# From up to down projection: the last block's product and sums on VectorE, two weight tiles placed elsewhere, two weight sums a step later

## The chip, the cores and the metric

One core of a Trainium2 chip runs the whole kernel in one launch. The core has TensorE (matrix products, PE in the profile, with the weight loads of its array as PEld), VectorE (DVE), ScalarE (ACT), GpSimd (POOL) and SyncE (SP), which here only issues DMAs. The metric is the device time of one execution in microseconds; the figure for the kernel before is the median of three runs.

## The reference

One layer of a diffusion backbone: a modulated norm, an mLSTM group and a windowed attention group, an output projection, and a channel mixer. The change lies in the channel mixer, for 1024 tokens, model width 1024 and hidden width 2816:

```python
def conv_glu(h, w_up, conv_w, conv_b, w_down):
    a, val = jnp.split(h @ w_up, 2, axis=-1)
    a = jax.nn.gelu(dwconv(a, conv_w, conv_b))
    return (a * val) @ w_down
...
        x = x + g_f * conv_glu(modulate(rmsnorm(x, norm_ffn[l]), sh_f, sc_f),
                               w_up[l], ffn_conv_w[l], ffn_conv_b[l], w_down[l])
...
    return rmsnorm(x, final_norm)
```

## The kernel before

**Up projection.** The 22 blocks of 128 hidden columns run in the loop over `i` from line 1773 on. For each block TensorE makes the gate and value rows, VectorE adds the parts and applies the convolution's taps, ScalarE does the gelu, and the product gate times value is made in two halves of 512 tokens: `mul1` on VectorE (line 1724) and `mul2` on GpSimd (line 1727), both into the block's tile `tt`. A block is held back by one turn, so the product of block 20 is made while TensorE works on block 21. The last block, `i = NF - 1 = 21`, is finished behind the loop, at lines 1904 to 1928.

**What is stored.** The down projection is done by a Strassen-like scheme with seven products instead of eight, so it needs sums of quarters of the hidden activation. `combine` (line 1730) stores a block's halves to DRAM and, for the second block of each couple, makes three sums on GpSimd, stores each (s1, s2, s4), with the partner block's tile `p` as room. It stores with `put`, which issues a DMA on SP. The helpers `add` (line 1496) and `sub` (line 1210) give the sums their lines in the profile. The third sum writes `tt[:, h1]`, the half that the a11/a12 store reads.

**Down projection.** Seven products follow in the order m1, m6, m2, m7, m5, m4, m3. Each goes through 11 blocks of 128 rows of weights, taken in six pairs (the sixth has one block). One pair of one product is a *step*, numbered n = 0 to 41, six to a product: m1 is steps 0 to 5, m6 is 6 to 11. A step is 24 matmuls (12 for a sixth pair): for each block of the pair and each of four row groups, three matmuls (line 2032), because both operands are split into a high and a low half. The first matmul of the three takes high and high, the second the low half of the weights (`dl`), the third the low half of the left operand (`al`).

A step's operands are prepared ahead, in an order that is written out by hand for TensorE, VectorE, ScalarE, GpSimd and SP alike, each of which works through it in order. In step n:

- `load(n + 4)` issues the weight load and the loads of the left operand (tiles `ar`, three of them in rotation) on SP;
- `cut(n + 2)` splits: ScalarE casts to the high half (line 1372: `dh` for weights, `ah` for the left operand), VectorE subtracts it from the source (line 1373: `dl`, `al`). At step 0 nothing is cut: the operands of steps 0 to 2 are split before the loop, those of step 3 in step 1.

**Weight sums.** m6, m7 and m4 use sums and differences of weight quarters. The dictionary `sums` says at which step the sum of pair j is due: steps 2, 3, 4, 6, 7, 8 for pairs 0 to 5. Two steps before its key, the loads of `b22[j]` and of a row tile `br` are issued, 512 KB each (256 KB for the sixth pair); at the key, behind the cut, VectorE subtracts `br` from `b22[j]`; a step later, ahead of the cut, it adds `b22[j]` to `b11[j]`, which m6 takes from step 6 + j on.

**Memory.** Weight tiles `b11` of pairs 4 and 5 and all six `b22` lie in the pool `gt`. It begins where the up projection's split weights ended and covers the bytes of that stage's working tiles (`u2`, `u3`, `av`, `sn`, `tt`, `vt`, `s3`) and, further on, of the hidden input `hB`. A load into such bytes waits until their last reader is done. The order of allocation sets which tile lies where.

Of the kernel before, what the change touches and what calls it, by code (L numbers as in the profile page):

```python
# [13 lines left out]
ALU = mybir.AluOpType  # L14
# [18 lines left out]
NF = FF // P  # L33
# [45 lines left out]
def build(tc, I, out, dbg=None):  # L79
    nc = tc.nc  # L80
    dbg = dbg or {}
    V, S, G, T = nc.vector, nc.scalar, nc.gpsimd, nc.tensor
# [991 lines left out]
    class Wout:  # L1074
# [32 lines left out]
        def add(self, n):  # L1107
            ns = slice(512 * n, 512 * n + 512)
            V.tensor_tensor(out=self.xb[:, ns], in0=self.po[:], in1=self.xb[:, ns], op=ALU.add)
            if n == 1:  # L1110
                nc.sync.dma_start(x2_d[self.b][:], self.xb[:])
# [98 lines left out]
    sub = lambda e, o, x, y: e.tensor_tensor(out=o, in0=x, in1=y, op=ALU.subtract)  # L1210
# [62 lines left out]
    add = lambda e, o, x, y: e.tensor_tensor(out=o, in0=x, in1=y, op=ALU.add)  # L1273
# [15 lines left out]
    for t in range(n + 2):  # L1289
# [3 lines left out]
        if t in WOT:  # L1293
            k = 4 + WOT.index(t)
# [201 lines left out]
    add = lambda e, o, x, y: e.tensor_tensor(out=o, in0=x, in1=y, op=ALU.add)  # L1496
# [87 lines left out]
    f = ExitStack()  # L1584
# [84 lines left out]
    h1, h2_ = slice(0, 512), slice(512, 1024)  # L1669

    class Block:
# [52 lines left out]
            V.tensor_tensor(out=self.tt[:, h1], in0=self.a[:], in1=self.tt[:, h1], op=ALU.mult)  # L1724

        def mul2(self):
            G.tensor_tensor(out=self.tt[:, h2_], in0=self.vt[:], in1=self.tt[:, h2_], op=ALU.mult)  # L1727


        def combine(self):  # L1730
            tt, put = self.tt, lambda n, src: nc.sync.dma_start(act_d[n, self.m % KD][:], src)
            put(("a11", "a12")[self.m >= KD], tt[:, h1])
            if self.m < KD:
                s3 = fs.tile([P, 512], F32, name="s3", tag="s3", bufs=1)
                sub(G, s3[:], tt[:, h1], tt[:, h2_])
                put("s3", s3[:])
                return
            put("a22", tt[:, h2_])
            p = self.before.tt
            add(G, p[:, h2_], p[:, h2_], tt[:, h2_])  # L1740
            put("s1", p[:, h2_])
            sub(G, p[:, h1], p[:, h2_], p[:, h1])
            put("s2", p[:, h1])
            sub(G, tt[:, h1], tt[:, h1], p[:, h1])
            put("s4", tt[:, h1])

    def wblock(k, d, kt):
# [113 lines left out]
    NP = len(PAIRS)  # L1861
    pair = lambda pool, n, **kw: pool.tile([P, 2, 512], F32, name=n, **kw)
    b11 = [er] + [pair(gb, f"b11_{k}") for k in range(1, 4)]
# [69 lines left out]
    gt = g.enter_context(tc.tile_pool(name="gt", bufs=1, reuse_waits="tile"))  # L1933
# [1 line left out]
    bank = [pD.tile([P, 512], F32, name=f"pd{i}") for i in range(8)]  # L1935

    bank = [[bank[i] for i in sl] for sl in ((1, 2, 7, 3), (5, 6, 4, 0))]
    b11 += [pair(gt, f"b11_{k}") for k in range(4, NP)]
    b22 = [pair(gt, f"b22_{k}") for k in range(NP)]
    gfr = go.tile([P, D], F32, name="gfr")  # L1940
    fnr = go.tile([P, D], F32, name="fnr")
    us = [go.tile([P, 512], F32, name=f"us{i}") for i in range(4)]
# [90 lines left out]
                     skip_group_check=not fresh)  # L2033

    todo = []
    sums = {(2, 3, 4, 6, 7, 8)[j]: j for j in range(NP)}
    rows = {}
    for t, (p, ps, fresh) in enumerate(products):
        for j in range(NP):
# [12 lines left out]
            if n - 1 in sums:  # L2052
                k = sums[n - 1]
                m = len(PAIRS[k])
                add(V, b11[k][:, 0:m], b22[k][:, 0:m], b11[k][:, 0:m])
            if n + 2 in raws:
                q, k = steps[n + 2]
# [10 lines left out]
            if n in sums:  # L2068
                k = sums[n]
# [125 lines left out]
```

## Time and profile before

| what | value |
|---|---|
| median of three runs | 1264.26 us (1264.09 to 1265.34) |
| profiled execution, its own time | 1263.85 us |
| its span, first to last instruction | 1262.1 us |
| granted TensorE clock, mean | 0.999 |
| first matmul of the down projection starts at | 1043.68 us |
| last matmul of the down projection starts at | 1254.5 us |

The times in the profile count from the start of the span. A row of the instructions in order of time gives start, duration, engine, line, operation, output and inputs with their shapes, and in brackets how long the engine was idle before it and what ended that idle time. A row of the chain of work gives start, duration, engine or DMA and the tile. A row of the windows gives, for a stretch, its length, then the busy time of PE, PEld, DVE, ACT and POOL with the count of instructions, the granted clock, the share of DMA engines in use and GB/s. Matmuls are pipelined: their durations overlap, so a matmul's lateness is read from the distance of the starts.

### The profile page before, as it was taken

To read this page: it belongs to the slowest core of one execution; us is meant where nothing else is said; L and a number is where in the kernel's file an instruction comes from. 1 tells how busy PE (TensorE), PEld (TensorE's weight loads), DVE (VectorE), ACT (ScalarE), POOL (GpSimd) and SP (SyncE) were. 2 spreads that over 40 slices of the span, in tenths; PEclk is the share of its full clock that TensorE was granted. 3 is DMA by queue.
4 is the path that set the end of the run, shared out by engine and by line. 5 is a ranking of instruction groups with operands and counts; after the bars stand their busy time and mean duration, and the time that the engine had idled before them with its cause. 6 is when DMAs were issued, how large, how long until landed. Compare 5 with 4: busy or idle time off the path is not lost.

```text
span 1262.1 us, 19247 instructions
## 1 busy us (share of the span) xinstructions
PE 1233.2 (98%) x7044; PEld 1059.5 (84%) x7044; DVE 973.4 (77%) x1691; ACT 638.8 (51%) x1310; POOL 187.5 (15%) x162
## 2 busy tenths in 40 slices
PE   6999999999999999999999999999999999999997
PEld 4799999999898888888887888888888888788886
DVE  5863777777887888788987877777777777877887
ACT  6732556464865777776843333333333334434435
POOL 1200000000001444221002232133231232001000
PEclk9999999999999999999999999999999999999999
DMA  9541635352254333104314322223322237975563
GB/s 360 190 138 35 151 117 152 119 178 68 85 176 165 128 126 110 51 34 167 117 51 133 116 98 104 93 101 116 103 105 100 94 136 269 335 252 187 192 195 134
DMA packets 90560, 176.17 MB, mean 140 GB/s; under 512 B 12954, under 2 KB 29538, under 8 KB 90466
## 3 DMA queue, kind: packets, MB, share of 16 engines
q1 hardware_dynamic: 90178, 174.15, 41.1%
q8 instruction: 56, 0.92, 0.3%
q10 hardware_dynamic: 288, 0.79, 0.2%
q14 instruction: 38, 0.31, 0.1%
HBM read 136.58 MB, written 38.33 MB: 139 GB/s over the span
## 4 chain that ended last, share of the span: by engine, by line
PE 80%; DVE 7%; ACT 5%; DMA 5%; issue 2%; SPq 1%; POOL 1%; ACTq 0%; DVEq 0%; POOLq 0%
PE pd L2032 14%; PE pa L1492 8%; PE pc L1492 8%; PE pp L600 7%; PE pe L1492 4%; PE pd L1492 4%; PE pb L1492 4%; PE u L1194 3%; PE pv L305 2%; PE pv L307 2%; PE pv L306 2%; DMA wa<-in_w_ada_dram 2%; PE pt L1171 2%; PE po L305 2%; PE po L307 1%
## 5 line engine op out<-in xcount | busy, mean ns | idle before, releaser
L1609 ACT CAST wh<-Rb 128x1024 fp32r<-128x1024 f32 (+1 forms) x63 | 56.8, 903 | 144.4 <-PE pd L1492 77.3
L2032 PE MATMUL pd<-dh,al 128*128 128x512 f32 x296 | 115.4, 390 | 0.8 <-DVE al L1373 0.8
L2032 PE MATMUL pd<-dl,ah 128*128 128x512 f32 x296 | 115.3, 389 | 0.0
L2032 PE MATMUL pd<-dh,ah 128*128 128x512 f32 x296 | 115.2, 389 | 0.0
L1492 PE MATMUL pc<-hB,wh 128*128 128x512 f32 x344 | 105.5, 389 | 0.0
L1492 PE MATMUL pa<-hB,wh 128*128 128x512 f32 x336 | 103.7, 390 | 0.3 <-ACT sn L1691 0.2
L1210 DVE TENSOR_TENSOR wl<-Rb,wh 128x1024 fp32r<-128x1024 f32 (+1 forms) x63 | 65.8, 1046 | 39.2 <-ACT wh L1609 38.6
L1727 POOL TENSOR_TENSOR tt<-vt,tt 128x512 f32<-128x512 f32 x22 | 29.5, 1343 | 367.5 <-ACT tt L1721 367.5
L600 PE MATMUL pp<-hl,wh 128*128 128x512 f32 x256 | 79.3, 405 | 0.0
L305 PE MATMUL pv<-wh,hl 128*128 128x256 f32 x256 | 75.9, 296 | 0.0
L1492 PEld LDWEIGHTS pc<-hB,wh 128*128 128x128 f32 x344 | 64.6, 188 | 13.4
L1492 PEld LDWEIGHTS pa<-hB,wh 128*128 128x128 f32 x336 | 62.9, 188 | 14.0 <-ACT sn L1691 1.1
L307 PE MATMUL pv<-wh,hl 128*128 128x256 f32 x256 | 72.4, 283 | 0.0
L306 PE MATMUL pv<-wl,hl 128*128 128x256 f32 x256 | 72.3, 282 | 0.0
L1492 PE MATMUL pc<-hB,wl 128*128 128x512 f32 x172 | 66.4, 389 | 0.0
L2032 PEld LDWEIGHTS pd<-dh,al 128*128 128x128 f32 x296 | 55.6, 188 | 12.9 <-DVE al L1373 1.6
L2032 PEld LDWEIGHTS pd<-dl,ah 128*128 128x128 f32 x296 | 55.6, 188 | 12.0 <-DVE dl L1373 0.3
L1492 PE MATMUL pa<-hB,wl 128*128 128x512 f32 x168 | 65.4, 389 | 0.0
L2032 PEld LDWEIGHTS pd<-dh,ah 128*128 128x128 f32 x296 | 55.6, 188 | 11.6
L1178 ACT CAST ph<-pt 128x512 fp32r<-128x512 f32 (+1 forms) x88 | 46.2, 525 | 26.0 <-PE pt L1171 25.8
L1148 DVE TENSOR_REDUCE nm<-sps 128x1 f32<-128x641 f32 (+1 forms) x64 | 50.3, 786 | 4.9 <-PE sps L1144 3.4
L1492 PE MATMUL pd<-hB,wh 128*128 128x512 f32 x176 | 53.9, 390 | 0.0
(1095 smaller groups left out, 3692.1 us busy)
## 6 DMA issues: line engine op xcount, KB each, us to landing
w<-in_w_ada_dram SPq DMA_DIRECT2D x64, 256.0 KB, 2.7
br<-in_w_down_dram SPq DMA_DIRECT2D x25, 512.0 KB, 5.6
ar<-act_s SPq DMA_DIRECT2D x44, 256.0 KB, 3.2
Ra<-in_w_up_dram SPq DMA_DIRECT2D x21, 512.0 KB, 3.6
Rb<-in_w_up_dram SPq DMA_DIRECT2D x21, 512.0 KB, 3.6
act_a<-tt SPq DMA_DIRECT2D x33, 256.0 KB, 2.0
act_s<-tt SPq DMA_DIRECT2D x33, 256.0 KB, 2.0
wr<-in_w_h_dram SPq DMA_DIRECT2D x16, 512.0 KB, 5.1
```

The lines of the kernel that those rows point to most:

```text
L305: T.matmul(ps, st_hi, mv_hi, start=first, stop=False)
L306: T.matmul(ps, st_hi, mv_lo, start=False, stop=False)
L307: T.matmul(ps, st_lo, mv_hi, start=False, stop=last)
L600: T.matmul(pp[:, 512 * n:512 * n + 512], wkq[sw][:, kt, cs], hl[n][part][:, kt, :], start=kt == 0 and sw + part == 0, stop=kt == KT - 1 an ...
L1148: V.tensor_reduce(out=self.nm[:, j:j + 1], in_=self.sv[j], axis=AX.X, op=ALU.max, negate=True)
L1178: S.copy(self.ph[i][:, :w], self.pt[i][:, :w])
L1194: T.matmul(self.u[:], vv[:, c, self.g], part[i][:, kk * 2 * P:(kk + 1) * 2 * P], start=kb + m == 0, stop=kb == last and m == 1)
L1210: sub = lambda e, o, x, y: e.tensor_tensor(out=o, in0=x, in1=y, op=ALU.subtract)
L1492: T.matmul(ps[:, cols], wt[sw][:, j, kt * P:kt * P + P], hB[part][:, blk, kt, cols], start=first and n == 0, stop=last and n == len(seq) - ...
L1609: S.copy(wt[0][:], src)
L1727: G.tensor_tensor(out=self.tt[:, h2_], in0=self.vt[:], in1=self.tt[:, h2_], op=ALU.mult)
L2032: T.matmul(ps[:], ac[sa][:, js], w[sw], start=first and n == 0, stop=last and n == 2, skip_group_check=not fresh)
```

## The change

Three edits. In the last block alone, `mul2` and the three sums of `combine` run on VectorE instead of GpSimd; all other blocks stay. In the pool `gt`, the six `b22` tiles are allocated first, then `b11` of the sixth pair, then `b11` of the fifth. And the keys of `sums` change from 2, 3, 4, 6, 7, 8 to 2, 4, 5, 6, 7, 8, so that pairs 1 and 2 are due a step later: their loads are issued at steps 2 and 3, the subtractions fall in steps 4 and 5, the additions in steps 5 and 6.

```diff
         def mul2(self):
-            G.tensor_tensor(out=self.tt[:, h2_], in0=self.vt[:], in1=self.tt[:, h2_], op=ALU.mult)
+            e = V if self.i == NF - 1 else G
+            e.tensor_tensor(out=self.tt[:, h2_], in0=self.vt[:], in1=self.tt[:, h2_], op=ALU.mult)
...
             p = self.before.tt
-            add(G, p[:, h2_], p[:, h2_], tt[:, h2_])
+            e = V if self.i == NF - 1 else G
+            add(e, p[:, h2_], p[:, h2_], tt[:, h2_])
             put("s1", p[:, h2_])
-            sub(G, p[:, h1], p[:, h2_], p[:, h1])
+            sub(e, p[:, h1], p[:, h2_], p[:, h1])
             put("s2", p[:, h1])
-            sub(G, tt[:, h1], tt[:, h1], p[:, h1])
+            sub(e, tt[:, h1], tt[:, h1], p[:, h1])
             put("s4", tt[:, h1])
...
-    b11 += [pair(gt, f"b11_{k}") for k in range(4, NP)]
     b22 = [pair(gt, f"b22_{k}") for k in range(NP)]
+    b11 += [pair(gt, f"b11_{k}") for k in range(NP - 1, 3, -1)][::-1]
...
-    sums = {(2, 3, 4, 6, 7, 8)[j]: j for j in range(NP)}
+    sums = {(2, 4, 5, 6, 7, 8)[j]: j for j in range(NP)}
```

## The prediction

> **What bounds the kernel now.** I read the page first, then the chain of work that ended last, then TensorE's instructions in order of time where that chain leaves TensorE.
>
> ```profile
> span 1262.1 us, 19247 instructions
> PE 1233.2 (98%) x7044; PEld 1059.5 (84%) x7044; DVE 973.4 (77%) x1691; ACT 638.8 (51%) x1310; POOL 187.5 (15%) x162
> ...
> 1049.60 2.20 POOL tt L1727
> 1051.88 2.16 POOL tt L1496
> 1054.12 1.62 POOL tt L1210
> 1055.81 1.63 POOL tt L1210
> 1058.84 4.97 DMA ar<-act_a
> 1063.83 8.12 DMA ar<-act_s
> 1075.52 175.98 PE pd L2032 x775
> ```
>
> TensorE sets the time. The chain leaves it only around the hand-over from up to down projection: the last block's product and sums on GpSimd (POOL), then two loads of left operands, then TensorE in one piece for 176 us. So the change can win only what TensorE loses here, and the chain does not say how much that is. The start of each matmul does (start, duration):
>
> ```profile
> 1049.12 0.39 PE L2032 MATMUL pd<-dh,ah 128*128 128x512 f32 x1
> ...
> 1065.67 0.39 PE L2032 MATMUL pd<-dl,ah 128*128 128x512 f32 x1
> 1066.25 0.50 PE L2032 MATMUL pd<-dh,al 128*128 128x512 f32 x1 [0.19 <-DVE al L1373]
> 1066.59 0.39 PE L2032 MATMUL pd<-dh,ah 128*128 128x512 f32 x1
> ...
> 1074.10 0.39 PE L2032 MATMUL pd<-dh,ah 128*128 128x512 f32 x1
> 1074.38 0.49 PE L2032 MATMUL pd<-dl,ah 128*128 128x512 f32 x1
> 1075.52 0.50 PE L2032 MATMUL pd<-dh,al 128*128 128x512 f32 x1 [0.64 <-DVE al L1373]
> 1075.86 0.39 PE L2032 MATMUL pd<-dh,ah 128*128 128x512 f32 x1
> ```
>
> From 1049.12 to 1065.67 lie 73 starts, so the pitch is 16.55/73 = 0.2267 us. Above it: 1066.25 and 1066.59 come 0.35 and 0.11 late, then 1074.38, 1075.52 and 1075.86 come 0.05, 0.91 and 0.11 late: **1.53 us**. A second reading: step 1 starts at 1049.12, a step is a pair of weight blocks, 24 matmuls (12 for the odd sixth), so the third matmul of step 6 is 110 pitches after 1049.12, due at 1074.06; it came 1.46 late, and 0.11 follow: 1.57. I take **1.55 us**, in two stalls: 0.47 at step 4 (m1's fifth pair), 1.08 at step 6 (m6's first). Both end with `al`, the low half of the left operand.
>
> **The change, part by part.**
>
> *Product and three sums to VectorE (DVE).* What they feed is SP's in-order queue: five stores, then the loads of step 4 and on.
>
> ```profile
> 1051.27 0.88 SPq L1731 DMA_DIRECT2D act_a<-tt  x2
> 1054.06 3.71 SPq L1731 DMA_DIRECT2D act_s<-tt  x3
> 1057.83 0.43 SPq L1877 DMA_DIRECT2D b<-in_w_down_dram  x1
> ...
> 1063.16 1.00 SPq L1881 DMA_DIRECT2D ar<-act_s  x2
> ...
> 1050.56 0.68 DVE L1724 TENSOR_TENSOR tt<-pa,tt 128x512 f32<-128x512 f32 x1
> 1051.16 1.73 DVE L1373 TENSOR_TENSOR dl<-b,dh 128x1024 fp32r<-128x1024 f32 x1
> 1052.81 3.47 DVE L1373 TENSOR_TENSOR al<-a,ah 128x512 fp32r<-128x512 f32 x2
> 1063.58 1.23 DVE L1373 TENSOR_TENSOR dl<-b,dh 128x1024 fp32r<-128x1024 f32 x1 [7.30 <-ACT dh L1372]
> 1064.97 1.23 DVE L1373 TENSOR_TENSOR al<-ar,ah 128x1024 fp32r<-128x1024 f32 x1 [0.17 <-ACT ah L1372]
> ...
> 1094.94 0.69 DVE L1496 TENSOR_TENSOR b<-b,b 128x512 f32<-128x512 f32 x1
> ...
> DMA to landing us min/median/max: 2.0/2.0/2.8
> ```
>
> The load of step 4 (1057.83) goes out right behind the last store, and that waited for POOL's last sum (1055.81 + 1.63 = 1057.44). On VectorE, behind the first product (ends 1051.24), four instructions of the 0.69 us row: product to 1051.9, first sum to 1052.6, second to 1053.3. The third writes the half of `tt` that the a12 store still reads, an added wait: issued at 1051.27, these stores (last line: issue to landing) land after 2.0 to 2.8, so 1053.3 to 1054.1. The third sum ends at 1054.0 to 1054.8; I take 1054.8, so stores and loads go out **2.6 us earlier** (3.4 at the other bound).
>
> Queued behind the waiting sum is the split of step 3's operands: 1.23 + 0.69 + 0.69 from 1054.8, done at 1057.4. TensorE needs its first `al` at 1049.12 + 50 pitches = 1060.46: 3.1 us to spare. That cover, and the 7.30 us in which VectorE now waits, is why I cost the 4 x 0.69 = 2.76 us at nothing.
>
> VectorE's 1.73 and 3.47 above, against 1.23 and 0.69 alone, lie beside POOL's 1.62 to 2.20. The Trainium skill (SBUF — State Buffer, Who interferes with whom) says that a VectorE instruction with two SBUF inputs contends with a GpSimd instruction that reads SBUF. By that rule the split shrinks once POOL is empty, as I took it, and this trace agrees (1.73 beside POOL, 1.23 without); were it to stay at 1.73 + 3.47, it would end at 1060.0, still ahead of 1060.46, and the sum stays.
>
> *Step 4 after.* Its `al` ended at 1064.97 + 1.23 = 1066.20, due at 1049.12 + 74 pitches = 1065.90. All before it waited for the loads; 2.6 earlier it ends at 1063.6. The 0.47 goes.
>
> *Weight sums later.* The text of the diff moves two: pairs 1 and 2, from steps 3 and 4 to 4 and 5. With each go two 512 KB loads (issued two steps ahead), a subtraction in that step and an addition in the next. So pair 1's two loads move past the left operand of step 6.
>
> ```profile
> 1072.04 1.05 ACT L1372 CAST ah<-ar 128x1024 fp32r<-128x1024 f32 x1 [1.78 <-DMA ar<-act_s]
> ...
> 1070.71 1.23 DVE L1210 TENSOR_TENSOR b<-b,br 128x1024 f32<-128x1024 f32 x1 [0.41 <-DMA br<-in_w_down_dram]
> 1071.97 1.23 DVE L1496 TENSOR_TENSOR b<-b,b 128x1024 f32<-128x1024 f32 x1
> ...
> 1074.25 1.22 DVE L1373 TENSOR_TENSOR al<-ar,ah 128x1024 fp32r<-128x1024 f32 x1
> ...
> 1060.00:1070.00 10.00, 9.81 (x43) 7.80 (x42) 5.80 (x6) 4.14 (x5) 0.00 (x0) 1.00 1.02 363
> ```
>
> The DMA engines are full here (share 1.02, 363 GB/s), so 1.05 MB fewer ahead is 2.9 us. Step 6's `al` ended at 1075.47, due 1074.06. With its load 2.6 earlier it would end at 1072.9; with the reorder alone at 1072.6; with both at 1070.0. VectorE too has pair 1's 1.23 + 1.23 no longer ahead of it. Either edit removes the 1.08, so it is robust.
>
> What is late next: behind step 6's `al` at 1070.0 come pair 1's two instructions (1072.5), ScalarE's 1.05 cast (1073.5), the two splits of step 7 (1075.9), due at 1074.06 + 24 pitches = 1079.5. Pair 2 the same way: step 8's `al` at about 1081.9, due 1084.9. Three us remain; from there VectorE's order is the old one.
>
> *Another place.* From the tiles' sizes, the fifth pair moves to bytes of the hidden input `hB`, whose last reader is the up projection's last matmul, the sixth beside the last block's value tile, and the b22 tiles slide down, off the stored ones for pairs 0 to 2. Nothing to win by itself: the old fifth load went out 0.06 after the stores (1054.06 + 3.71 = 1057.77). Bounds: 0, and one store's landing, 2.8, where a tile still lay under a store. I take 0, by the 0.06.
>
> *Sum.* 0.47 + 1.08 = 1.55 off the profiled execution: 1263.85 (span 1262.1 and 1.75 around it) becomes 1262.30. That execution is 0.41 below the median 1264.26, so the forecast is 1264.26 - 1.55 = **1262.7 us**. Behind TensorE's last matmul the tail keeps its length: it starts when TensorE ends.
>
> **The rivals.**
>
> *VectorE takes the gain back later.* The next tight point:
>
> ```profile
> 1135.24 1.06 ACT L1372 CAST dh<-b 128x1024 fp32r<-128x1024 f32 x1 [0.71 <-PE pd L2032]
> ...
> 1193.07 1.22 DVE L1373 TENSOR_TENSOR al<-ar,ah 128x1024 fp32r<-128x1024 f32 x1
> ```
>
> The product m4 begins four products of 132 matmuls after m6; its first `al`, done at 1193.07 + 1.22 = 1194.29, is due 528 pitches after 1075.52, at 1195.2: 0.9 to spare. If this run of VectorE did not move, 1.55 - 0.9 = 0.65 would return: 1263.4. Against it: the run's last outside release is TensorE itself (1135.24), so it moves along. The same figure covers one stall of two left standing (1264.26 - 0.47 = 1263.8 at worst). Chance 0.12.
>
> *VectorE as the bound.* The Trainium skill (Perfetto Trace Analysis, Optimizing Scalar/DVE Operations) advises moving work from a saturated VectorE to other engines, the opposite of this. As a mechanism here: the 2.76 us are not absorbed and reach 1195.2, where 0.9 are spare: 1.86 stall against 1.55 won, 1264.6. The trace does not bear it out: the 7.30 us wait is VectorE without work at this very place. Chance 0.03.
>
> *Slower: VectorE held by the a12 store.*
>
> ```profile
> 1050.00:1055.00 5.00, 5.00 (x23) 4.13 (x22) 5.00 (x5) 1.50 (x3) 4.84 (x3) 1.00 0.31 114
> ```
>
> If that store lands late, the third sum, step 3's split and the last store all wait. It decides from a landing at 1060.46 - 0.69 - 1.23 - 0.69 = 1057.85, that is 6.6 us after issue. At the 8.12 us that the `act_s` load took, the sum starts at 1059.4 and the split ends at 1062.0: TensorE loses 1.5 at step 3. The last store goes out at 1060.1, 2.6 later than now, so step 4's `al` ends at 1068.8, due at 1067.4 by then: 1.4 more. Step 6 is covered by the reorder (1075.47 + 2.6 - 2.9 = 1075.2, due at 1077.0). 2.9 lost instead of 1.55: 1265.6, and each us of landing beyond that adds one; 0.2% over before is passed at 9.3. Against: 2.8 is the longest store here, and the DMA engines are light just then (share 0.31 in this stretch). Chance 0.04.
>
> *The change does nothing*, because the stalls come back from the full DMA engines: 1264.3. Chance 0.03.
>
> **How the numbers follow.** Forecast 0.78, the others 0.12, 0.03, 0.04, 0.03. Under 0.2% (2.5 us) a measurement of this kernel cannot tell from no change; the forecast is inside it. More than 1.55 cannot be won here, and only scatter (three runs spread 1.25 us) reaches 1261.7: faster 0.06. Slower needs 1266.8: the third rival from a landing of 9.3 on, or one I do not see: 0.06. Same: 0.88. Range: 1262.1 (a gain of 1.55 and half the runs' spread) to 1264.3 (the second and last rivals, nearly): 0.8.
>
> **What would show it.** No POOL work between 1036 and 1140; four VectorE instructions of 0.69 us between 1051 and 1055, a gap before the last; the fifth pair's load near 1055; matmul starts 0.227 apart through steps 4 and 6; TensorE's last piece from the up projection on without a break. Wrong if a matmul at step 3, 7 or 8, or the first of m4, starts late for `al`, or if SP waits between the last store and the fifth pair's load.

## The result, and the profile after

| | median | runs |
|---|---|---|
| before | 1264.43 us | 22 (1263.76 to 1265.59) |
| changed | 1262.79 us | 22 (1261.90 to 1264.66) |
| ratio | 0.9987 | 95% interval 0.9982 to 0.9993 |

The change saves 0.13%, about 1.6 us. That is inside the 0.2% that the prediction counted as no change, yet with 22 runs of each kernel the interval lies clear of 1. Where the chain of work of the changed kernel passes from the up to the down projection (start, duration, engine, tile):

```profile
1041.52 2.72 PE pc L1492 x12
1044.24 206.05 PE pd L2034 x909
```

GpSimd and the two loads are gone from it: TensorE passes from the up projection into the down projection without a step aside and stays on the chain for 206 us, up to the tail (the profile's line numbers are shifted by one behind the first edited line and by two behind the second; a few matmul records are missing). SP's DMA issues, then VectorE's instructions, in order of time, changed kernel:

```profile
1051.80 0.92 SPq L1732 DMA_DIRECT2D act_a<-tt  x2
1053.19 1.77 SPq L1732 DMA_DIRECT2D act_s<-tt  x3
1055.02 0.44 SPq L1879 DMA_DIRECT2D b<-in_w_down_dram  x1
...
1058.75 1.46 SPq L1883 DMA_DIRECT2D ar<-act_s  x2
```

```profile
1051.09 0.68 DVE L1724 TENSOR_TENSOR tt<-pa,tt 128x512 f32<-128x512 f32 x1
1051.69 0.68 DVE L1728 TENSOR_TENSOR tt<-vt,tt 128x512 f32<-128x512 f32 x1
1052.47 0.69 DVE L1496 TENSOR_TENSOR tt<-tt 128x512 f32<-128x512 f32 x1
1053.20 1.42 DVE L1210 TENSOR_TENSOR tt<-tt 128x512 f32<-128x512 f32 x2
1054.54 1.22 DVE L1373 TENSOR_TENSOR dl<-b,dh 128x1024 fp32r<-128x1024 f32 x1
1055.67 1.28 DVE L1373 TENSOR_TENSOR al<-a,ah 128x512 fp32r<-128x512 f32 x2
1061.03 1.22 DVE L1373 TENSOR_TENSOR dl<-b,dh 128x1024 fp32r<-128x1024 f32 x1 [4.07 <-ACT dh L1372]
1062.38 1.23 DVE L1373 TENSOR_TENSOR al<-ar,ah 128x1024 fp32r<-128x1024 f32 x1
```

TensorE's matmuls where the stalls of steps 4 and 6 were (in each group the second row is the step's first matmul that needs `al`):

```profile
1066.06 0.39 PE L2034 MATMUL pd<-dl,ah 128*128 128x512 f32 x1
1066.29 0.39 PE L2034 MATMUL pd<-dh,al 128*128 128x512 f32 x1
1066.52 0.39 PE L2034 MATMUL pd<-dh,ah 128*128 128x512 f32 x1
...
1074.22 0.39 PE L2034 MATMUL pd<-dl,ah 128*128 128x512 f32 x1
1074.45 0.39 PE L2034 MATMUL pd<-dh,al 128*128 128x512 f32 x1
```

The down projection starts at 1043.68 in the profile before and at 1044.08 here, so the two are compared by the distance from that start. (It lies between 1043.68 and 1045.03 in all ten profiles, also where nothing ahead of it was changed, as in e2_sums at 1044.34.) The fifth pair's load goes out 10.94 us behind it instead of 14.15, that is 3.2 us earlier. Step 4's `al` ends at 1063.61, 19.53 behind; its matmul is due 98 pitches behind the start, at 22.2. From the first start of the down projection to the last row of its matmuls TensorE takes 208.76 us instead of 210.36: 1.60 less. (That row holds the last three matmuls, so it starts two pitches ahead of the last start.) What lies behind it, up to the end of the span, is about 8 us in both.

### The profile page after: what moved, and what is told of

Same layout as the page of the kernel before. It is cut to its first block, busy times and chain, and to the rows that moved or that the text cites. A ratio compares the mean times of both kernels' runs of the same rounds, so it can differ in the third digit from the quotient of the medians.

```text
span 1260.9 us, 19246 instructions
## 1 busy us (share of the span) xinstructions
PE 1234.0 (98%) x7044; PEld 1060.3 (84%) x7044; DVE 973.1 (77%) x1695; ACT 638.5 (51%) x1310; POOL 179.9 (14%) x158
## 4 chain that ended last, share of the span: by engine, by line
PE 85%; DVE 6%; ACT 5%; DMA 2%; issue 2%; SPq 1%; ACTq 0%; DVEq 0%
PE pd L2034 16%; PE pc L1492 9%; PE pa L1492 9%; PE pp L600 7%; PE pe L1492 5%; PE pd L1492 4%; PE pb L1492 4%; PE u L1194 3%; PE pv L305 2%; PE pv L307 2%; PE pv L306 2%; PE pt L1171 2%; PE po L305 2%; PE po L307 1%; PE po L306 1%
```

## The experiments

All times are ratios to the kernel before, run on the same chip. The other columns are read from each run's profile: the issue of the fifth pair's load, counted from the first matmul of the down projection; the lateness of matmul starts above the pitch, by step; and the time from the first start of the down projection to its last row. Its floor, with no late start, is 208.76. Starts less than 0.04 us late are left out, so the late starts add up to as much as 0.1 less than the last column has above the floor.

| kernel | ratio, 95% interval | load at | late starts (us) | first start to last row |
|---|---|---|---|---|
| before | | 14.15 | step 4: 0.46, step 6: 1.07 | 210.36 |
| changed | 0.9987 (0.9982 to 0.9993) | 10.94 | none | 208.76 |
| e1_vector | 0.9991 (0.9982 to 1.0000) | 10.65 | none | 208.76 |
| e2_sums | 0.9994 (0.9985 to 1.0003) | 14.31 | step 4: 0.66, step 10: 0.28 | 209.79 |
| e3_place | 0.9997 (0.9988 to 1.0006) | 14.45 | step 4: 0.86, step 6: 1.06 | 210.75 |
| e4_product | 1.0004 (0.9995 to 1.0013) | 14.36 | step 4: 0.71, step 6: 1.02 | 210.56 |
| e5_four_more | 0.9990 (0.9981 to 1.0000) | 13.85 | step 4: 0.33, step 10: 0.30 | 209.47 |
| e6_eight_more | 1.0011 (1.0002 to 1.0020) | 16.31 | step 3: 1.02, step 4: 1.71, step 10: 0.34 | 211.94 |
| e7_early_sums | 0.9985 (0.9976 to 0.9994) | 10.59 | none | 208.76 |
| e8_five_in_m5 | 1.0003 (0.9993 to 1.0012) | 10.77 | first step of m4: 2.13 | 210.93 |

The ratios alone part few of these kernels, since the intervals reach 0.9 per thousand either way; what follows rests on the late starts, which are read from one profile of each kernel.

### e1_vector: product and sums on VectorE, nothing else

```diff
-            G.tensor_tensor(out=self.tt[:, h2_], ...
+            e = V if self.i == NF - 1 else G
+            e.tensor_tensor(out=self.tt[:, h2_], ...
...
-            add(G, p[:, h2_], p[:, h2_], tt[:, h2_])
+            e = V if self.i == NF - 1 else G
+            add(e, p[:, h2_], p[:, h2_], tt[:, h2_])
```

(and both subtractions likewise)

> Only the product and the three sums of the last block go to VectorE; weight sums and places stay as before. Theory (both TensorE stalls hang on the time of the last store, so this edit alone is enough): no late matmul at steps 4 and 6, down projection 1.6 to 1.8 us shorter, about 1262.7. Rival (step 6 needs the reorder of the loads too): the 0.47 of step 4 goes, the 1.08 of step 6 stays, about 1263.8. Rival (places: without the move SP waits between the last store and the loads of the weight sums): a gap on SP and a late step 6, about 1263.8.

No matmul is late, and the down projection takes 208.76, as with all three edits. Its chain has the same one piece; then SP's last stores and the fifth pair's load, and TensorE's matmuls at step 6:

```profile
1044.31 206.05 PE pd L2034 x909
```

```profile
1052.98 1.77 SPq L1732 DMA_DIRECT2D act_s<-tt  x3
1054.80 0.44 SPq L1879 DMA_DIRECT2D b<-in_w_down_dram  x1
```

```profile
1074.29 0.39 PE L2034 MATMUL pd<-dl,ah 128*128 128x512 f32 x1
1074.52 0.39 PE L2034 MATMUL pd<-dh,al 128*128 128x512 f32 x1
```

By the profile this edit is the whole gain; the ratio, 0.9991, agrees within its interval. Neither rival holds: step 6 does not need the reorder, and no place needs to change (SP goes from the last store to the load in 0.05 us).

### e2_sums: weight sums a step later, nothing else

```diff
-    sums = {(2, 3, 4, 6, 7, 8)[j]: j for j in range(NP)}
+    sums = {(2, 4, 5, 6, 7, 8)[j]: j for j in range(NP)}
```

> Only the weight sums of pairs 1 and 2 a step later. Theory: GpSimd still ends at the same time, so the stall of step 4 (0.47) stays; the left operand of step 6 comes about 2.9 us earlier and its stall (1.08) goes: about 1263.2. Rival (the full DMA engines bring it back elsewhere): a late matmul at step 7 or 8, about 1264.4.

TensorE's matmuls in order of time, at the two places where a start is late:

```profile
1066.33 0.39 PE L2032 MATMUL pd<-dl,ah 128*128 128x512 f32 x1
1067.11 0.50 PE L2032 MATMUL pd<-dh,al 128*128 128x512 f32 x1 [0.40 <-DVE al L1373]
...
1096.96 0.39 PE L2032 MATMUL pd<-dl,ah 128*128 128x512 f32 x1
1097.37 0.50 PE L2032 MATMUL pd<-dh,al 128*128 128x512 f32 x1
```

Step 4's stall stays and step 6's is gone, as the theory had it. But the second pair of rows is new: a start 0.18 late at step 10, and 0.10 more behind it. The rival that the gain would come back was right in kind, at a step that nobody had named. VectorE shows why (same kernel; the first two rows are the split of step 6, the others the turns of steps 9 and 10):

```profile
1071.16 1.23 DVE L1373 TENSOR_TENSOR dl<-er,dh 128x1024 fp32r<-128x1024 f32 x1
1072.30 1.22 DVE L1373 TENSOR_TENSOR al<-ar,ah 128x1024 fp32r<-128x1024 f32 x1
...
1089.01 1.22 DVE L1373 TENSOR_TENSOR dl<-b,dh 128x1024 fp32r<-128x1024 f32 x1 [1.19 <-ACT dh L1372]
1090.15 1.22 DVE L1373 TENSOR_TENSOR al<-ar,ah 128x1024 fp32r<-128x1024 f32 x1
1091.29 1.22 DVE L1210 TENSOR_TENSOR b<-b,br 128x1024 f32<-128x1024 f32 x1
1092.54 1.22 DVE L1496 TENSOR_TENSOR b<-b,b 128x1024 f32<-128x1024 f32 x1
1094.95 1.23 DVE L1373 TENSOR_TENSOR dl<-b,dh 128x1024 fp32r<-128x1024 f32 x1 [1.19 <-ACT dh L1372]
1096.10 1.22 DVE L1373 TENSOR_TENSOR al<-ar,ah 128x1024 fp32r<-128x1024 f32 x1
```

With a subtraction and an addition between two splits, a turn of VectorE takes 1094.95 - 1089.01 = 5.94 us: four instructions and a wait of 1.19 for ScalarE to cast the sum that was just made. A step of TensorE takes 24 x 0.2267 = 5.44. Each such turn comes 0.5 later against TensorE. The old order has a break, steps 7 and 8 are split without a sum between; the new one has none from step 6 to step 10.

### e3_place: order of the tiles, nothing else

```diff
-    b11 += [pair(gt, f"b11_{k}") for k in range(4, NP)]
     b22 = [pair(gt, f"b22_{k}") for k in range(NP)]
+    b11 += [pair(gt, f"b11_{k}") for k in range(NP - 1, 3, -1)][::-1]
```

> Only the order of the weight tiles in memory. Theory: nothing waits for a place before, so both stalls stay as they were: 1264.4, the fifth pair's load still right behind the last store. Rival (place matters): the loads of the weight sums go out earlier and step 6 is less late, 0.3 us or more.

Both stalls are there, and step 6's is what it was (1.06 and 1.07). Step 4's is larger (0.86 and 0.46), and the load goes out 0.30 later; in e2_sums and e4_product, which leave the places alone, it goes out 0.16 and 0.21 later and step 4 loses 0.66 and 0.71, so this is no mark of the place. The place of the tiles is worth nothing alone, and by e1_vector nothing beside the first edit either.

### e4_product: the product on VectorE, the sums on GpSimd

```diff
-            G.tensor_tensor(out=self.tt[:, h2_], ...
+            e = V if self.i == NF - 1 else G
+            e.tensor_tensor(out=self.tt[:, h2_], ...
```

> Only the last block's product goes to VectorE, its three sums stay on GpSimd. Theory (the end of the last sum decides): the product is ready at about the same time, 1051.9 by the trace before, the three sums of 1.6 to 2.2 us follow, the last store goes out within 0.3 us of before and both stalls stay: 1264.2 to 1264.4. Rival (the shared work of VectorE and GpSimd decides, and less on GpSimd is worth its share): a quarter of the gain or more, 1264.0 or less.

GpSimd, then VectorE, in order of time:

```profile
1052.76 2.11 POOL L1496 TENSOR_TENSOR tt<-tt 128x512 f32<-128x512 f32 x1 [16.64 <-DVE tt L1728]
1054.95 3.31 POOL L1210 TENSOR_TENSOR tt<-tt 128x512 f32<-128x512 f32 x2
```

```profile
1051.91 0.68 DVE L1728 TENSOR_TENSOR tt<-vt,tt 128x512 f32<-128x512 f32 x1
1052.51 1.22 DVE L1373 TENSOR_TENSOR dl<-b,dh 128x1024 fp32r<-128x1024 f32 x1
1053.64 3.48 DVE L1373 TENSOR_TENSOR al<-a,ah 128x512 fp32r<-128x512 f32 x2
```

The product takes 0.68 instead of 2.20 but ends no earlier (8.29 us behind the start of the down projection, 8.12 before), because on VectorE it comes behind that block's `mul1`. The three sums still end 1058.26 - 1044.30 = 13.96 us behind that start (1057.44 - 1043.68 = 13.76 before). Nothing is won. It is the end of the last sum that counts, not how much is moved: with load and stores no earlier, the stalls stay.

### e5_four_more and e6_eight_more: how wide the cover is

```diff
             e.tensor_tensor(out=self.tt[:, h2_], in0=self.vt[:], in1=self.tt[:, h2_], op=ALU.mult)
+            for _ in range(4 if e is V else 0):
+                add(V, self.vt[:], self.vt[:], self.vt[:])
```

(8 in the second)

> The changed kernel with four additions of 128x512 more on VectorE between the last block's product and its sums (they write a tile that nothing reads any more). Theory: about 2.8 us of delay against 2.85 us that step 4's low half has to spare in the changed kernel: 0 to 0.3 us lost, the time of the changed kernel. Rival (VectorE is the bound): 2.8 us lost, about 1265.6.

> The changed kernel with eight such additions more: 5.7 us of delay. Theory: past the cover, step 3's first low half is about 1.1 us late and step 4's about 1.8 on top, nothing at step 6: about 2.9 us lost, 1265.7, slower than before. Rival (VectorE is the bound): all 5.7 lost, about 1268.5. Rival (the cover is wider than read): nothing lost.

With four more, step 4 is 0.33 late and step 10 0.30: 0.71 us more than the floor, where 0 to 0.3 was expected; the part at step 10 had not been foreseen, and is the one that e2_sums shows. With eight more (TensorE's matmuls at the larger late starts, then VectorE's additions and the two subtractions):

```profile
1061.83 0.50 PE L2036 MATMUL pd<-dl,ah 128*128 128x512 f32 x1 [0.39 <-DVE dl L1373]
...
1068.35 0.50 PE L2036 MATMUL pd<-dh,ah 128*128 128x512 f32 x1 [0.65 <-ACT ah L1372]
...
1069.61 0.50 PE L2036 MATMUL pd<-dh,al 128*128 128x512 f32 x1 [0.53 <-DVE al L1373]
```

```profile
1052.81 5.78 DVE L1496 TENSOR_TENSOR vt<-vt 128x512 f32<-128x512 f32 x8
...
1059.22 1.42 DVE L1210 TENSOR_TENSOR tt<-tt 128x512 f32<-128x512 f32 x2
```

The additions take 5.78 us, and the load goes out 16.31 - 10.94 = 5.37 later than in the changed kernel. Steps 3 and 4 lose 1.02 + 1.71 = 2.73 of that, so the cover, the delay that costs nothing, is 2.6 us. With step 10 the whole loss is 211.94 - 208.76 = 3.18, and the kernel ends slower than before (1.0011). The table's column of the load says the same across all these kernels: with the load at 10.6 to 10.9 step 4 is on time, at 13.85 to 14.45 it is 0.33 to 0.86 late, at 16.31 steps 3 and 4 lose 2.73 together. Going back from that point one for one, the lateness begins with the load about 13.6 us behind the start, which fits the five kernels between to about 0.1 us, with the sums on GpSimd or on VectorE alike.

### e7_early_sums: the changed kernel with the old steps of the sums

```diff
-    sums = {(2, 4, 5, 6, 7, 8)[j]: j for j in range(NP)}
+    sums = {(2, 3, 4, 6, 7, 8)[j]: j for j in range(NP)}
```

> The changed kernel with the weight sums at their old steps (2, 3, 4, 6, 7, 8). Theory: step 6's low half ends about 2.9 us later than in the changed kernel and has 4.5 to spare there: no late matmul, the time of the changed kernel. Rival (the reorder carries step 6): 1.08 us back.

The time of the changed kernel, and again 208.76. The last `al` of VectorE's tight run, that of step 10, in the changed kernel and then in this one:

```profile
1092.65 1.22 DVE L1373 TENSOR_TENSOR al<-ar,ah 128x1024 fp32r<-128x1024 f32 x1
```

```profile
1090.74 1.22 DVE L1373 TENSOR_TENSOR al<-ar,ah 128x1024 fp32r<-128x1024 f32 x1
```

It is due 230 pitches behind the start: 1044.08 + 52.1 = 1096.2 in the changed kernel, 2.3 to spare; 1044.75 + 52.1 = 1096.9 here, 4.9 to spare. So beside the first edit the reorder wins nothing, and leaves 2.6 us less cover at step 10.

### e8_five_in_m5: the next tight point

```diff
+            for _ in range(5 if n == 4 * NP + 4 else 0):
+                add(V, tmp_()[:], gfr[:, 0:512], fnr[:, 0:512])
             if n + 2 in raws:
                 q, k = steps[n + 2]
```

> The changed kernel with five additions of 128x512 more on VectorE in the fifth step of m5, ahead of the split of m4's first operands (they write a tile that nothing reads). Theory: the first low half of m4 has 1.25 us to spare in the changed kernel, so about 3.1 us of delay loses about 1.8 at the first step of m4: 1264.5. Rival (VectorE has room there): nothing lost. Rival (its whole run is the bound): 3.1 lost.

```profile
1194.63 0.39 PE L2034 MATMUL pd<-dh,ah 128*128 128x512 f32 x1
1195.98 0.51 PE L2034 MATMUL pd<-dl,ah 128*128 128x512 f32 x1 [0.97 <-DVE dl L1373]
1197.12 0.50 PE L2034 MATMUL pd<-dh,al 128*128 128x512 f32 x1 [0.63 <-DVE al L1373]
```

```profile
1191.70 3.09 DVE L1496 TENSOR_TENSOR tm<-gfr,fnr 128x512 f32<-128x512 f32 x5
```

3.1 us of VectorE lose 2.1 at the first step of m4, 0.3 more than expected. The expectation took 1.25 to spare in the changed kernel; counted with the right first start (due at 1044.08 + 662 pitches = 1194.1, ready at 1193.05) it is 1.1, and restarting TensorE takes 0.1 more.

## Why the prediction was right

**The bound and the size.** TensorE is the bound, and its stalls at steps 4 and 6 were all there was to win: 1.55 was read from the starts, 1.60 is the difference of the two down projections, about 1.6 that of the medians. All of it is gone, and the tail moved along unchanged. One profile fixes the size less well than two decimals suggest: in the kernels that leave the sums on GpSimd and the reorder out, the two stalls came to 1.53 (before, load 14.15 us behind the start), 1.73 (e4_product, 14.36) and 1.92 us (e3_place, 14.45). That 1262.7 was forecast and 1262.79 measured is therefore in part luck.

**Product and sums to VectorE.** Right, and the whole cause (e1_vector). The four instructions cost nothing, as put: VectorE still waits 4.07 us ahead of step 4's split, where it waited 7.30. Loads and stores were put 2.6 us earlier with 3.4 as the other bound; 3.2 were measured. The added wait for the a12 store was priced high: the two subtractions took 1.42 us together, against 2 x 0.69 on their own, so the gap that was expected before the last of the four is not there. In e6_eight_more, where they start 7 us behind that store's issue, they take the same 1.42. The split of step 3 took 1.22 and 1.28 us instead of 1.73 and 3.47. That the 3.47 comes from GpSimd's sums is borne out by e4_product (3.48 with them); the 1.73 is not a matter of GpSimd being busy alone, for beside its first sum the same subtraction took 1.22 there. No time of TensorE hung on this: step 3 had room either way.

**Weight sums later.** "Either edit removes the 1.08" is shown: e1_vector has no stall at step 6 without the reorder, e2_sums none without the move to VectorE. The 2.9 us came from the DMA engines' share alone. Counted from the start of the down projection, step 6's `al` ends at 31.79 before and at 29.18 in e2_sums, 2.6 earlier, and at 28.37 in e7_early_sums and 25.99 in the changed kernel, 2.4 earlier. In e2_sums that split follows the one ahead of it on VectorE without a wait for the load (the row at 1071.16 has no idle time), so what ends last there is VectorE's own run, and no run here measures the DMA engines' part by itself.

The step that was short is "Three us remain; from there VectorE's order is the old one". What remains in the changed kernel is 3.9 us at step 7, 3.4 at step 8, 2.8 at step 9 and 2.3 at step 10: it shrinks by 0.5 us per step, because the turns of 5.94 us now follow each other without a break. It cost the changed kernel nothing, and 0.3 us where the stage runs late (e2_sums, e5_four_more, e6_eight_more).

**Another place.** Right at 0 (e3_place alone; e1_vector beside the first edit).

**The rivals.** VectorE takes no gain back at m4: its run moved along with TensorE (1.0 us to spare before, 1.1 after), and e8_five_in_m5 shows that the point is as tight as read. VectorE held by the a12 store did not happen, and no run shows such a late store. What a late third sum would cost is shown: e6_eight_more holds it up with 5.78 us of additions and is slower than before, with losses at steps 3 and 4 (1.02 and 1.71) of the size that the expectation worked out, and 0.34 at step 10 that it did not.

## What to carry to other kernels

Where one engine runs almost without a break, read the starts of its instructions against its pitch: the sum of late starts is the most that an edit to what feeds it there can win, and each operand's end against its due time says how wide the cover is. Work moved to a busier engine was free here because that engine waited at that place, and it paid because it freed an in-order queue sooner; what counted was the end of the last instruction that the queue waits for. When work is put off by a step, compare the length of a turn with and without it over all following turns, not only the first two.

## What the runs showed of the hardware

In all runs with a stall, a stop of TensorE is followed by one more start that is 0.10 to 0.11 us late, where the next start is not itself a stop, so a stop costs that much beyond its cause.

With GpSimd busy on 128x512 sums, two of VectorE's subtractions of 128x512 operands took 3.47 us together (3.48 in e4_product), against 0.69 for one alone. In the kernel before GpSimd's sums of that size took 1.62 to 2.16 there and its product 2.20, against a median of 1.30 for the product over all 22 blocks. Which of two overlapping instructions is stretched goes, in these rows, with which began first. VectorE's subtraction that began at 1052.51 in e4_product, ahead of GpSimd's sum at 1052.76, took 1.22, as it does alone, and the sum took 2.11. The one that began at 1051.16 in the kernel before, while GpSimd's product was under way since 1049.60, took 1.73. The profile calls its spans of GpSimd rough, and no run here was made to test this order.
